# Two token tiles of a projection side by side in one PSUM bank

## The chip, the cores and the metric

The kernel runs on one core of one Trainium2 chip. The metric is the device time of one execution in microseconds. A profiled execution additionally leaves a trace of all engines: TensorE (PE, with its weight loads shown apart as PEld), VectorE (DVE), ScalarE (ACT), GpSimd (POOL) and SyncE (SP, which here issues DMAs).

## What is computed

Two layers of a bidirectional trunk over 512 tokens of 1024 features, in float32. The first layer mixes tokens with an SSD scan and an mLSTM scan, the second with a GLA scan; each is followed by a convolutional feed-forward network.

```
for i in range(DEPTH):                       # 2 layers
    h = _rmsnorm(x, norm_g[i, 0])
    if i % 2 == 0:
        h = _ssd_mlstm_mixer(h, ab_w_in, ...)    # z, xbc, dt, q, k, v, o, gates = split(h @ w_in)
    else:
        h = _gla_mixer(h, c_w_in, ...)           # q, k, v, r, g_lr = split(h @ w_in)
    x = x + _rmsnorm(h, norm_g[i, 1])
    f = _conv_ffn(_rmsnorm(x, norm_g[i, 2]), ...)
    x = x + _rmsnorm(f, norm_g[i, 3])
```

What matters here are the input projections `h @ w_in`. Of their column blocks, `z`, `v` and `o` of the first layer and `v` and `r` of the second are wanted with the tokens on the partitions; all others with the features on the partitions.

## The kernel before

Every projection is made in an emulated float32: activations and weights are each split into a high and a low part, and one product becomes three matmuls (`mm3`: high-high, high-low, low-high) that add into the same PSUM region.

The projections with tokens on the partitions are made by `nat_job` (line 452). One call takes 256 columns of weights and makes a tensor of 512 tokens by 256 columns, in four tiles `c` = 0 to 3 of 128 tokens. For a tile, the 128 tokens of `h` are the stationary operand and the 256 weight columns stream; over eight blocks of features that is 8 x 3 = 24 matmuls of 128x256. Then `post` reads the tile out of PSUM on ACT: `post_v` and `post_o` of `pair` (lines 979 and 984) with two activations of 128x128 each, `post_z` (line 795), `post_v` of layer two (line 1224) and `post_r` (line 1234) with one of 128x256.

There are 20 calls of `nat_job`, so 80 tiles and 40 pairs of tiles. In the order of `A_ORDER` = p0 x0 z0 p1 x1 z1 p2 p3 these are: `v` and `o` of head pair 0, two calls for `z0`, `v` and `o` of pair 1, two calls for `z1`, `v` and `o` of pairs 2 and 3; and in the second layer four calls of `v_proj` and four of `r_proj`. The texts below number the calls from 0 to 19 in this order.

PSUM has eight banks of 512 columns per partition, given out under three names: `pj` (2 banks, the projections), `ps` (3 banks) and `pm` (3 banks, the scans). Of `pj`, tile `c` of a `nat_job` takes one bank of 512 columns and fills 256 of them, so the two banks go back and forth from tile to tile. The jobs with features on the partitions (`run_full`: 128x512 matmuls) take banks of `pj` too.

Three streams are woven into one program by `weave` (line 47): `stream_a`, the projections, on TensorE; `stream_b`, the gates (`gate_rows`) and the SSD scan; `stream_c`, the mLSTM scan. The second layer weaves two head streams with its projections likewise. A scheduler then sets the final order of each engine by its own estimate of when things are ready, and each engine works through its instructions strictly in that order: an instruction that waits holds up all behind it on its engine. The scheduler also places the semaphore waits. In the profile all lines of the engines' calls are that of a helper, L105, so instructions are told apart by the names of their tiles: a matmul of `nat_job` is `pj<-hi,s` or `pj<-lo,s`, its read-out `s<-pj,scol`, `s<-pj,hcol` or `t<-pj,scol`.

Of the kernel before, what the change touches and what calls it, by code (L numbers as in the profile page):

```python
# [19 lines left out]
KD = 8  # L20
# [110 lines left out]
def kernel(ctx: ExitStack, tc: tile.TileContext, xin, wst, cst, dsk, gw2, out, life=None, plan=None):  # L131
# [25 lines left out]
    def ps(tag="ps"):  # L157
        uid[0] += 1
        return pp.tile([P, 512], F32, tag=tag, name=f"{tag}{uid[0]}", bufs=BANKS[tag])

    def pj():
        return ps("pj")
# [110 lines left out]
    def w_take(n, width=P):  # L273

        res = []
        for _ in range(n):
            c0 = wstate["unit"]
            i, o = divmod(c0, 1024)
            while len(wstate["ready"]) < i + 1 + W_AHEAD and wstate["next"] < NSLAB:
                w_prep()  # L280
            hi, lo = wstate["ready"][i]
            res.append((hi[:, o:o + width], lo[:, o:o + width]))
            wstate["unit"] += width
        return res

    def mm3(o, a, b, first, last, parts=False):

        (ah, al), (bh, bl) = a, b
        kw = {"skip_group_check": True} if parts else {}
        PE.matmul(o, ah, bh, start=first, stop=False, **kw)  # L290
        PE.matmul(o, ah, bl, start=False, stop=False, **kw)
        PE.matmul(o, al, bh, start=False, stop=last, **kw)

    def hp(on):
        return tc.high_priority() if on else nullcontext()
# [156 lines left out]
    def nat_job(h, post, hi=False):  # L452

        w = w_take(KD, 256)
        for c in range(NCH):
            o = pj()
            for k in range(KD):
                hh, hl = h[k]
                tk = slice(c * P, (c + 1) * P)
                mm3(o[:, :256], (hh[:, tk], hl[:, tk]), w[k], k == 0, k == KD - 1)  # L460
            with hp(hi):
                post(o[:, :256], c)
            yield

    def transpose(o, i, n=P):
# [163 lines left out]
    def mixer0(h, x_again, sc, chain_of):  # L629
# [164 lines left out]
        def z_proj(nb):  # L794
            def post_z(o, c):
                gg, hf = divmod(nb, 2)
                if hf == 0:
                    zt[c][gg] = st()
                zz = t256()
                S.activation(zz, o, AF.Identity, scale=sc.col[:, c:c + 1])  # L800
                th = t256()
                S.activation(th, zz, AF.Tanh, scale=0.5)
                V.scalar_tensor_tensor(zt[c][gg][:, hf * 256:(hf + 1) * 256], th, 1.0, zz, ALU.add, ALU.mult)
            yield from nat_job(h, post_z, False)
# [166 lines left out]
        def pair(i):  # L971
            yield from run_full([Job(h, post=post_cp(kT, 2 * i + e, P ** -0.5)) for e in range(2)])
            yield from run_full([Job(h, post=post_cp(qT, 2 * i + e, 1.0)) for e in range(2)])
            for e in range(2):
                vx[2 * i + e] = st(w=516).rearrange("p (c l) -> p c l", l=129)
                G.memset(vx[2 * i + e][:, :, 128:129], 1.0)
                ot[2 * i + e] = st()

            def post_v(o, c):
                for e in range(2):  # L980
                    S.activation(vx[2 * i + e][:, c, 0:P], o[:, e * P:(e + 1) * P], AF.Identity,
                                 scale=sc.col[:, c:c + 1])

            def post_o(o, c):
                for e in range(2):
                    S.activation(ot[2 * i + e][:, c * P:(c + 1) * P], o[:, e * P:(e + 1) * P], AF.Tanh,
                                 scale=hcol[:, c:c + 1])
            yield from nat_job(h, post_v, False)
            yield from nat_job(h, post_o, False)
            done.add(f"pair{i}")  # L990
# [617 lines left out]
```

## Time and profile before

| | |
|---|---|
| time, median of 3 runs (range) | 1539.5 us (1535.16 to 1539.62) |
| time of the profiled execution | 1537.51 us |
| its span, first to last instruction | 1535.8 us |
| PE busy | 1487.3 us, 97% of the span |
| PEld busy | 1305.5 us, 85% |
| DVE busy | 1157.0 us, 75% |
| ACT busy | 770.3 us, 50% |
| POOL busy | 141.1 us, 9% |
| HBM traffic | 104 GB/s over the span |
| mean granted TensorE clock | 0.989 |
| chain that ended last, by engine | PE 80%, DVE 13%, ACT 3%, issue 2%, DMA 2% |

How to read it. The chain is followed back from the last instruction, at each step to what released it or to the instruction ahead of it on its engine. The busy time of PE is modelled per matmul and matmuls overlap; a matmul's price is better read from start to start. The number in brackets behind a row of the timeline is the time for which the engine sat idle before it, and what ended that.

### The profile page before, as it was taken

Reading aid. Unit: us, or ns where it says so; the run is one execution under the profiler, and the core shown is the slowest. Engines: PE = TensorE matmul, PEld = TensorE weight load, DVE = VectorE, ACT = ScalarE, POOL = GpSimd, SP = SyncE. Lnnn points to the kernel's source line nnn. Section 1 sums busy time; section 2 is a strip of 40 time slices with the busy share of each in tenths; the row PEclk is TensorE's granted clock in tenths of the full one; section 3 lists DMA queues with packets and bytes.
Section 4 is the critical chain, followed back from the end, with each engine's and each line's share of the span. In section 5 each row is a group of like instructions: output and inputs, shape, how many; then the busy total and the mean of one; then the engine's idle time right before and its main releaser. Section 6 shows DMA issues by size and latency. Waiting matters only on the chain.

```text
span 1535.8 us, 23362 instructions
## 1 busy us (share of the span) xinstructions
PE 1487.3 (97%) x9008; PEld 1305.5 (85%) x9008; DVE 1157.0 (75%) x1975; ACT 770.3 (50%) x1420; POOL 141.1 (9%) x165
## 2 busy tenths in 40 slices
PE   7999998999999999999999999999999999999996
PEld 7889887887887988898898887899998889889876
DVE  7986889867764789868886686938537996889765
ACT  7445546653742655444444464637545554444433
POOL 4010311221110020000000020000003000000000
PEclk9999999999999999999999998999999999999998
DMA  6243334334331533143233432221233324222432
GB/s 199 88 160 91 107 97 127 106 93 132 110 120 47 173 98 122 55 138 97 69 105 121 137 116 90 82 70 56 69 120 128 110 69 132 89 86 77 141 94 72
DMA packets 76528, 160.96 MB, mean 105 GB/s; under 512 B 7280, under 2 KB 42112, under 8 KB 76416
## 3 DMA queue, kind: packets, MB, share of 16 engines
q1 hardware_dynamic: 66592, 149.97, 30.5%
q10 hardware_dynamic: 9360, 8.43, 1.8%
q8 instruction: 71, 1.16, 0.3%
q0 software_dynamic: 464, 1.06, 0.2%
q14 instruction: 41, 0.34, 0.1%
HBM read 150.62 MB, written 8.78 MB: 104 GB/s over the span
## 4 chain that ended last, share of the span: by engine, by line
PE 80%; DVE 13%; ACT 3%; issue 2%; DMA 2%; POOL 0%; DVEq 0%; SPq 0%; ACTq 0%; POOLq 0%
PE pj L105 33%; PE ps L105 24%; PE pm L105 23%; DVE s L105 9%; DVE lo L105 2%; ACT s L105 1%; DMA s<-rowd 1%; DVE t L105 1%; DVE pacc L105 1%; DMA raw<-in_w 0%; ACT hi L105 0%; POOL s L105 0%; DMA xsave<-s 0%; ACT t L105 0%; DVE sum L105 0%
## 5 line engine op out<-in xcount | busy, mean ns | idle before, releaser
L105 PE MATMUL pj<-s,hi 128*128 128x512 f32 (+1 forms) x1216 | 365.8, 382 | 3.5 <-ACT s L105 3.5
L105 DVE TENSOR_TENSOR lo<-raw,hi 128x1024 fp32r<-128x1024 f32 x202 | 250.8, 1246 | 111.1 <-ACT hi L105 110.6
L105 ACT CAST hi<-raw 128x1024 fp32r<-128x1024 f32 x202 | 210.6, 1047 | 213.4 <-PE pj L105 102.9
L105 PEld LDWEIGHTS pj<-s,hi 128*128 128x128 f32 x1216 | 221.6, 190 | 49.1 <-issue 5.1
L105 PE MATMUL pm<-s,hi 128*128 128x512 f32 (+1 forms) x928 | 251.6, 355 | 9.0 <-ACT s L105 7.8
L105 PE MATMUL pj<-hi,s 128*128 128x256 f32 x1280 | 243.3, 288 | 6.7 <-DVE s L105 3.7
L105 PE MATMUL ps<-s,hi 128*128 128x512 f32 (+1 forms) x928 | 245.7, 350 | 0.2 <-DVE t L105 0.2
L105 PE MATMUL pj<-s,lo 128*128 128x512 f32 (+1 forms) x608 | 230.6, 379 | 0.0
L105 PEld LDWEIGHTS pj<-hi,s 128*128 128x128 f32 x1280 | 201.6, 191 | 9.3 <-DVE s L105 4.1
L105 PEld LDWEIGHTS pm<-s,hi 128*128 128x128 f32 x928 | 164.8, 190 | 36.0 <-ACT s L105 8.7
L105 PEld LDWEIGHTS ps<-s,hi 128*128 128x128 f32 x928 | 161.7, 188 | 24.9 <-issue 0.3
L105 PE MATMUL pj<-lo,s 128*128 128x256 f32 x640 | 181.6, 284 | 0.0
L105 DVE TENSOR_TENSOR s<-s,s 128x512 f32<-128x512 f32 (+3 forms) x262 | 159.9, 630 | 18.9 <-ACT s L105 15.5
L105 DVE SCALAR_TENSOR_TENSOR s<-s,cc,s 128x511 f32<-128x511 f32 (+1 forms) x240 | 166.9, 712 | 5.3 <-ACT s L105 3.5
L105 PE MATMUL ps<-s,lo 128*128 128x512 f32 (+1 forms) x464 | 162.9, 351 | 1.2 <-DVE lo L105 1.2
L105 PE MATMUL pm<-s,lo 128*128 128x512 f32 (+1 forms) x464 | 163.4, 352 | 0.0
L105 ACT ACTIVATE s<-s 128x512 f32<-128x512 f32 (+2 forms) x153 | 91.3, 606 | 116.9 <-DVE s L105 105.2
L105 ACT ACTIVATE s<-s,cc 128x512 f32<-128x512 f32 (+2 forms) x188 | 120.7, 662 | 41.1 <-DVE s L105 39.9
L105 PEld LDWEIGHTS pj<-s,lo 128*128 128x128 f32 x608 | 115.7, 190 | 22.7 <-issue 1.3
L105 PEld LDWEIGHTS pj<-lo,s 128*128 128x128 f32 x640 | 122.5, 191 | 1.4 <-issue 1.0
L105 POOL TENSOR_TENSOR s<-s,s 128x512 f32<-128x512 f32 (+1 forms) x56 | 70.5, 1264 | 404.1 <-DVE s L105 235.6
L105 PEld LDWEIGHTS ps<-s,lo 128*128 128x128 f32 x464 | 87.3, 188 | 14.1 <-DVE lo L105 1.6
(659 smaller groups left out, 2102.0 us busy)
## 6 DMA issues: line engine op xcount, KB each, us to landing
raw<-in_w SPq DMA_DIRECT2D x234, 512.0 KB, 3.4
s<-rowd SPq DMA_DIRECT2D x64, 256.0 KB, 3.8
xmid<-s SPq DMA_DIRECT2D x32, 128.0 KB, 1.8
s<-xmid ACTq DMA_DIRECT2D x32, 128.0 KB, 2.7
s<-in_x SPq DMA_DIRECT2D x8, 256.0 KB, 5.8
s<-in_x ACTq DMA_DIRECT2D x16, 128.0 KB, 2.7
xsave<-s SPq DMA_DIRECT2D x16, 128.0 KB, 1.8
s<-xsave ACTq DMA_DIRECT2D x16, 128.0 KB, 2.6
```

The source lines that it names most:

```text
L105: return f(*a, **k)
```

## The change

`nat_job` asks for a bank only at every second tile. The even tile fills columns 0 to 255 of it, the odd tile columns 256 to 511. The number of matmuls, their shapes, the read-outs and their sizes stay as they are, and so do the numbers of banks given to each name; a call now takes two banks of `pj`, where it took four in turn.

```diff
         w = w_take(KD, 256)
         for c in range(NCH):
-            o = pj()
+            if c % 2 == 0:
+                bank = pj()
+            o = bank[:, c % 2 * 256:c % 2 * 256 + 256]
             for k in range(KD):
                 hh, hl = h[k]
                 tk = slice(c * P, (c + 1) * P)
-                mm3(o[:, :256], (hh[:, tk], hl[:, tk]), w[k], k == 0, k == KD - 1)
+                mm3(o, (hh[:, tk], hl[:, tk]), w[k], k == 0, k == KD - 1)
             with hp(hi):
-                post(o[:, :256], c)
+                post(o, c)
             yield
```

The scheduler makes another order of it. Three places show what moves.

On PE, in call 0 (`v` of pair 0), before: the second tile (`pj75`) ends, and the third (`pj76`) begins with a wait for the first tile's bank.

```order
L105 MATMUL pj75_695<-lo9_554,s24_156 128x256
L105 MATMUL pj75_695<-hi9_553,s25_157 128x256
L105 MATMUL pj76_722<-hi8_520,s10_128 128x256 [waits PE_49,Activation_49]
L105 MATMUL pj76_722<-lo8_521,s10_128 128x256
L105 MATMUL pj76_722<-hi8_520,s11_129 128x256
L105 MATMUL pj76_722<-hi8_520,s12_132 128x256
```

The same call after the change, where the first tile of bank `pj74` ends and the second tile of the same bank begins:

```order
L105 MATMUL pj74_668<-hi9_553,s25_157 128x256
L105 MATMUL pj75_721<-hi8_520,s10_128 128x256 [waits DVE_49]
L105 MATMUL pj75_721<-lo8_521,s10_128 128x256
L105 MATMUL pj75_721<-hi8_520,s11_129 128x256
L105 MATMUL pj75_721<-hi8_520,s12_132 128x256
L105 MATMUL pj75_721<-lo8_521,s12_132 128x256
L105 MATMUL pj75_721<-hi8_520,s13_133 128x256
L105 MATMUL pj74_668<-hi8_520,s10_128 128x256 [waits Activation_49]
L105 MATMUL pj74_668<-lo8_521,s10_128 128x256
```

What moved: the odd tile's first matmul now waits for ACT, whose last word on that bank is the read of the even tile that has just ended; six matmuls of the third tile (bank `pj75`) have been put between. Before, a whole tile of 24 matmuls lay between the end of a tile and the next use of its bank.

On ACT, in call 1 (`o` of pair 0), before: the reads of the first two tiles stand ahead of `dec`, a small activation of the gate rows that waits for DVE, and the third behind it.

```order
L105 ACTIVATE s71_652<-pj78_788,hcol61_516 128x128 [waits PE_49]
L105 ACTIVATE s73_655<-pj78_788,hcol61_516 128x128
L105 ACTIVATE s128_1253<-s128_1253 64x512 [waits DVE_49]
L105 ACTIVATE s71_652<-pj79_815,hcol61_516 128x128 [waits PE_49]
L105 ACTIVATE s73_655<-pj79_815,hcol61_516 128x128
L105 ACTIVATE dec129_1257<-ce127_1245 64x4
L105 ACTIVATE dec129_1257<-sC148_1394 64x4 [waits DVE_49]
L105 ACTIVATE s71_652<-pj80_842,hcol61_516 128x128 [waits PE_49]
L105 ACTIVATE s73_655<-pj80_842,hcol61_516 128x128
```

The same rows after the change:

```order
L105 ACTIVATE s71_652<-pj76_786,hcol61_516 128x128 [waits PE_49]
L105 ACTIVATE s73_655<-pj76_786,hcol61_516 128x128
L105 ACTIVATE s122_1247<-s122_1247 64x512 [waits DVE_49]
L105 ACTIVATE dec123_1251<-ce121_1239 64x4
L105 ACTIVATE dec123_1251<-sC140_1386 64x4 [waits DVE_49]
L105 ACTIVATE s71_652<-pj76_786,hcol61_516 128x128 [waits PE_49]
L105 ACTIVATE s73_655<-pj76_786,hcol61_516 128x128
L105 ACTIVATE s71_652<-pj77_839,hcol61_516 128x128 [waits PE_49]
L105 ACTIVATE s73_655<-pj77_839,hcol61_516 128x128
```

What moved: the second read of the call now stands behind `dec` too.

On PE, at the end of call 1, before: the fourth tile (`pj81`) ends, and the next job with features on the partitions (`pj95`, 128x512) waits for its bank, the one of the third tile.

```order
L105 MATMUL pj81_869<-lo11_620,s24_156 128x256
L105 MATMUL pj81_869<-hi11_619,s25_157 128x256
L105 MATMUL pj95_944<-s10_128,hi12_658 128x512 [waits PE_49,Activation_49]
L105 MATMUL pj95_944<-s11_129,hi12_658 128x512
L105 MATMUL pj95_944<-s10_128,lo12_659 128x512 [waits DVE_49]
```

After the change, from the end of the call's second tile (`pj76`) to the begin of its fourth:

```order
L105 MATMUL pj76_786<-hi11_619,s25_157 128x256
L105 MATMUL pj77_839<-lo11_620,s24_156 128x256
L105 MATMUL pj77_839<-hi11_619,s25_157 128x256
L105 MATMUL ps144_1406<-ident_74,s81_915 128x128 [waits DVE_49]
L105 MATMUL ps144_1406<-ident_74,s81_915 128x128 x3
L105 MATMUL ps145_1412<-ident_74,s82_916 128x128 [waits DVE_49]
L105 MATMUL pj91_940<-s10_128,hi12_658 128x512 [waits PE_49,Activation_49]
L105 MATMUL pj91_940<-s11_129,hi12_658 128x512
L105 MATMUL pj77_839<-hi10_586,s10_128 128x256 [waits Activation_49]
L105 MATMUL pj77_839<-lo10_587,s10_128 128x256
```

What moved: the call's fourth tile (the lower `pj77` rows) stands behind two matmuls of the next job, whose bank waits for the read of the second tile, and five transposes of the gate rows stand ahead of that wait.

## Rows read from the trace of the kernel before

**Rows 1.** The page: busy time by engine, and the chain by engine.

```profile
PE 1487.3 (97%) x9008; PEld 1305.5 (85%) x9008; DVE 1157.0 (75%) x1975; ACT 770.3 (50%) x1420; POOL 141.1 (9%) x165
...
PE 80%; DVE 13%; ACT 3%; issue 2%; DMA 2%; POOL 0%; DVEq 0%; SPq 0%; ACTq 0%; POOLq 0%
```

**Rows 2.** Waits of PE: us in total, times, longest us.

```profile
PE pj L105 <- ACT s L105: 5.3, 4, 3.5
PE pj L105 <- DVE s L105: 3.7, 2, 2.1
```

**Rows 3.** The chain in order of time (start, us): two tiles of `nat_job` back to back.

```profile
192.80 5.75 PE pj L105 x48
```

**Rows 4.** Timeline (start us, us): ends of tiles in calls 0 and 3.

```profile
63.49 0.40 PE L105 MATMUL pj<-hi,s 128*128 128x256 f32 x2
...
63.81 0.63 ACT L105 ACTIVATE s<-pj,scol 128x128 f32<-128x128 f32 x2 [2.02 <-PE pj L105]
...
119.67 0.40 PE L105 MATMUL pj<-hi,s 128*128 128x256 f32 x2
...
119.98 0.47 ACT L105 ACTIVATE t<-pj,scol 128x256 f32<-128x256 f32 x1 [1.11 <-PE pj L105]
```

**Rows 5.** Timeline: the end of call 1.

```profile
86.35 0.20 ACT L105 ACTIVATE dec<-sC 64x4 f32<-64x4 f32 x1 [7.56 <-DVE sC L105]
86.57 0.63 ACT L105 ACTIVATE s<-pj,hcol 128x128 f32<-128x128 f32 x2
...
87.25 0.73 PE L105 MATMUL pj<-s,hi 128*128 128x512 f32 x2 [3.51 <-ACT s L105]
```

**Rows 6.** Timeline: call 4, end of its third tile.

```profile
179.28 0.28 PE L105 MATMUL pj<-hi,s 128*128 128x256 f32 x1
179.40 1.88 PE L105 MATMUL ps<-s,s 128*128 128x512 f32 x4
...
182.08 0.61 ACT L105 ACTIVATE s<-pj,scol 128x128 f32<-128x128 f32 x2
```

**Rows 7.** Timeline: call 6, end of its third tile, and the begin of call 7.

```profile
259.05 0.40 PE L105 MATMUL pj<-hi,s 128*128 128x256 f32 x2
...
263.00 0.46 ACT L105 ACTIVATE t<-pj,scol 128x256 f32<-128x256 f32 x1
...
263.50 0.38 PE L105 MATMUL pj<-hi,s 128*128 128x256 f32 x1 [1.32 <-ACT t L105]
```

**Rows 8.** Timeline: ends of the third tiles of calls 8 and 9.

```profile
328.29 0.28 PE L105 MATMUL pj<-hi,s 128*128 128x256 f32 x1
...
330.31 0.60 ACT L105 ACTIVATE s<-pj,scol 128x128 f32<-128x128 f32 x2
...
342.69 0.28 PE L105 MATMUL pj<-hi,s 128*128 128x256 f32 x1
...
344.85 0.61 ACT L105 ACTIVATE s<-pj,hcol 128x128 f32<-128x128 f32 x2
```

**Rows 9.** Timeline: call 10, end of its first tile.

```profile
386.85 0.28 PE L105 MATMUL pj<-hi,s 128*128 128x256 f32 x1
...
389.25 0.58 PE L105 MATMUL pj<-hi,s 128*128 128x256 f32 x1 [2.12 <-DVE s L105]
...
392.23 0.40 ACT L105 ACTIVATE s<-s,s 128x128 f32<-128x128 f32 x1 [1.92 <-DMA s<-rowd]
392.53 0.61 ACT L105 ACTIVATE s<-pj,scol 128x128 f32<-128x128 f32 x2
```

**Rows 10.** Timeline: call 12, end of its third tile, and the begin of call 13.

```profile
978.22 0.40 PE L105 MATMUL pj<-hi,s 128*128 128x256 f32 x2
...
981.74 0.46 ACT L105 ACTIVATE s<-pj,scol 128x256 f32<-128x256 f32 x1
...
982.25 0.39 PE L105 MATMUL pj<-hi,s 128*128 128x256 f32 x1 [0.90 <-ACT s L105]
```

**Rows 11.** Windows: stretch, length, busy us (x) of PE, PEld, DVE, ACT, POOL, PEclk, DMA.

```profile
389.04:392.44 3.40, 3.19 (x15) 3.19 (x16) 3.19 (x8) 1.48 (x6) 0.00 (x0) 0.50 0.58 150
```

## The prediction

> **What bounds the kernel now.** I read the page first. PE is busy for 97% of the span and makes 80% of the chain that ended last [rows 1], so a microsecond in which PE stands still is a microsecond of the time, except in the fifth of the chain that runs over DVE, ACT and DMAs. Next the waits of PE: those before matmuls into `pj` are short and few, 5.3 us for ACT and 3.7 us for DVE [rows 2]. Then the chain in order of time, for the price of the work that the change touches: 48 matmuls of 256 columns, two tiles, take 5.75 us [rows 3], so 0.12 us a matmul and 2.87 us a tile. Last the timeline at the ends of tiles [rows 4 to 10], where the reader is to see how long after a tile's last matmul ACT has finished reading it. In a row with x2 the first of the two is the tile's last matmul, and the other already belongs to the next tile.
>
> **What the change removes and adds.** The matmuls and the reads are the same, so there is no work to price. Only waits move. Before, a bank came back after a whole tile on the other bank, 2.87 us; that sufficed nearly everywhere. Now the odd tile goes into the bank that ACT is just reading, and by the new order its first matmul waits for that read. What PE does meanwhile is what the scheduler has put between: the rows of the order count as cover, at 0.12 us each for matmuls of 256 columns. So for each of the 40 odd tiles the price is (end of ACT's read of the even tile, plus 0.05 us until PE starts, as from 87.20 to 87.25 [rows 5]) less (start of the even tile's last matmul, plus 0.12 us, plus the cover). That the wait guards the whole bank and not the columns is what the order shows; in the trace of before no matmul writes a bank that is being read. The Trainium skill says the same of the chip, in "PSUM — Partial Sum Buffer", section "PSUM bank collisions raise a hardware error": TensorE and a reader must be kept apart by bank and quadrant of partitions, not by address. By that rule the odd tile must wait, and the sum is the one below; by a rule on columns it would not wait at all and the sum would be zero.
>
> **Odd tiles where ACT is idle.** A read of two activations ends 0.95 us after the tile's last matmul begins (63.49 to 64.44), one of a single activation 0.78 us (119.67 to 120.45) [rows 4]; PE could go on after 1.00 and 0.83 us. The order gives call 0 six matmuls of cover, so 7 x 0.12 = 0.84 us, a wait of 0.16 us; nine further tiles, in calls 2, 3 and 12 to 16, have five, 0.72 us, a wait of 0.11 us. Together 2 x 0.16 + 9 x 0.11 = 1.3 us. This is the floor, and it has one answer.
>
> **Call 1.** Before, PE had all four tiles done and idled for 3.51 us until ACT, held by `dec` waiting for DVE, had read the third tile at 87.20 [rows 5]. In the new order the second read stands behind `dec` as well, and the fourth tile behind a wait for it. The gate rows on DVE do not hang on these tiles, so `dec` comes when it came; then at 87.25 PE has a whole tile left, 2.87 us, and meets a further wait of some 0.2 us, as two activations of together 0.63 us read the third tile while two matmuls run. The five transposes that now fall into the idle time give back some 0.6 us. Net 2.5 us.
>
> **Tiles where ACT is late.** Here the read of an even tile was late and nobody cared.
> - Call 4, third tile: last matmul at 179.28, read done at 182.69 [rows 6]. The cover is two float32 matmuls of 512 columns, four records of together 1.88 us, which end at 181.28, and one short matmul. Wait 182.74 - 181.3 = 1.4 us.
> - Call 6, third tile: last matmul at 259.05, read done at 263.46 [rows 7]. Cover seven matmuls: until 260.0. Wait 3.5 us, of which PE already spent 1.32 us before call 7. Net 2.2 us.
> - Calls 8 and 9, third tiles: 328.29 to 330.91, and 342.69 to 345.46 [rows 8]. For the first the cover is eight short matmuls, at least 9 x 0.12 = 1.1 us, so at most 1.6 us are left; I take 1.3. For the second it is the same pair as in call 4, 2.0 us from the last matmul on, so 0.8 us; I take 1.0, as the pair's records overlap.
> - Call 10, first tile: ACT waits for the landing of a row of `rowd` until 392.23 and reads the tile until 393.14 [rows 9]. Before, PE went on at 389.25 with the second tile; now it cannot before 393.19. What it did in that time at half clock (PEclk 0.50 in [rows 11]) was all but two matmuls of a tile, 22 x 0.12 = 2.6 us at full clock. Net 2.6 us, as long as the DMA lands when it landed.
> - Call 12, third tile: 978.22 to 982.20 [rows 10]. Cover seven matmuls, until 979.2. Wait 3.1 us, of which 0.90 us was there before. Net 2.2 us.
>
> The remaining 22 odd tiles have a longer cover or an even tile that was read early. Some reads of calls 5, 11 and 13 were late too, but by an ACT that in the new order has caught up while PE waited a tile earlier; I take zero, and up to 6 us for the upper end (that each costs again what calls 4, 10 and 12 cost: 1.4 + 2.6 + 2.2).
>
> **The clock.** In the 3.40 us from 389.04, behind PE's idle 2.12 us, the granted clock is 0.50, the lower of its two levels, 1.2 instead of 2.4 GHz [rows 9, 11]; such a stretch costs half of itself, 1.7 us. The new waits of calls 1, 6, 10 and 12 are longer than 2.12 us; calls 1 and 10 had the idle time and call 6 the smaller part of it. I count one stretch more than before, +1.7 us, with none to six for the range.
>
> **The sum.** 1.3 + 2.5 + 1.4 + 2.2 + 1.3 + 1.0 + 2.6 + 2.2 = 14.5 us, with the clock 16.2 us. From this I take 1 us, as a PE that comes later finds DVE and ACT further on, and a few of its other waits (each 0.4 to 2 us) shrink. Against the profiled execution, 1537.5 us, that gives 1552.7; the median of the runs, 1539.5, lies 2.0 above it, so the forecast for the median is 1539.5 + 15.2, some **1555 us**.
>
> **Rivals.**
> - *All waits in full.* ACT does not catch up (+6.2), the idle time already there in calls 6 and 12 is not credited (+2.2), and six waits of over 1 us drop the clock instead of one (+8.5): 15.2 + 16.9 = 32, so 1572 us. For it: the waits come in clusters within one mixer. Against: ACT is busy half of the time only [rows 1]. The Trainium skill, "TensorE: Matmul & The Clock Gate", section "A second HAM failure mode: psum-queue depth-cycling", tells of a kernel whose short idle times between PSUM banks kept bringing the clock down and up; that is this rival's mechanism, and 389 us is the place of before that agrees.
> - *The delays are absorbed.* The waits fall where the chain runs over DVE and ACT, and only the floor and call 1's remainder stay: 1.3 to 4 us, 1541 to 1543 us. For it: a fifth of the chain is not PE's, and the lateness in calls 8 to 10 comes from DMAs and DVE that PE may find further on. Against: PE has 97% and hardly any waits to give back.
> - *Faster: the bank comes back two tiles later.* When PE changes the bank, the other bank's last read now lies a tile and a half back, so the waits of PE before `pj` go, 5.3 + 3.7 us [rows 2], and two half-clock stretches behind them, 3.4 us: less 12.4, plus the floor 1.3, gives 1539.5 - 11 = 1528 us. It decides at ACT's lateness: it holds if ACT reads an even tile within the cover of 0.7 to 0.8 us. Rows 6 to 10 speak against it, and so does the order in call 1, where the 3.51 us wait stays.
> - That the odd tile does not wait after all is excluded by the order: it names ACT in 39 of 40 cases.
>
> **How the numbers follow.** A measurement of this kernel can tell some 0.3% from no change, 4.6 us. The forecast, +5 to +25 us, gets 0.65; all waits in full, above that, 0.17; absorbed, 0.13; faster, 0.05. So faster 0.05, same 0.13, slower 0.82. For 8 in 10 the range takes in the forecast's own, half of the absorbed case and most of the case in full: 1541 to 1574 us.
>
> **What would show it.** Right: the timeline of the changed kernel has PE idle at the seams inside a bank, released by ACT's read of `pj`, with PE's waits for `s` and `t` of ACT before `pj` summing to some 20 to 25 us instead of 5.3 [rows 2]; seams of calls 14 to 16 show 0.1 us; call 1's fourth tile stands behind 87 us. PE's busy time grows only by half-clock stretches. Wrong: such waits stay below 8 us in total (ACT had caught up everywhere), or PE's other waits shrink by as much as these grow.

## The result, and the profile after

The changed kernel takes 1554.26 us (median of 4 runs, 1548.81 to 1554.61), the kernel before beside it 1537.33 us (4 runs, 1533.68 to 1539.62). The ratio is 1.0106, with a 95% interval of 1.0087 to 1.0126: slower by 13 to 19 us. The forecast was 1555 us, slower, in a range of 1541 to 1574.

The profiled execution took 1554.04 us, with a span of 1552.3; before it was 1537.51 and 1535.8. From the page of after: busy time by engine; the chain by engine; and the costliest group on PE (busy us, mean ns of one | idle us just before it, and what ended most of that).

```profile
PE 1493.4 (96%) x9008; PEld 1307.5 (84%) x9008; DVE 1158.8 (75%) x1975; ACT 770.9 (50%) x1420; POOL 140.8 (9%) x165
...
PE 77%; DVE 13%; ACT 4%; DMA 3%; issue 2%; POOL 1%; SPq 0%; DVEq 0%; ACTq 0%; POOLq 0%
...
L105 PE MATMUL pj<-hi,s 128*128 128x256 f32 x1280 | 248.4, 290 | 17.2 <-ACT s L105 11.5
```

The work is the same to the instruction [rows 1], yet PE is busy for 6.1 us more and stands still for some 10 us more (a sum over all its gaps of 49.5 us instead of 39.8). The 1280 matmuls of this group now have 17.2 us of idle time in front of them. The waits of PE before `pj` name the cause (us in total, times, longest us); they answer to [rows 2]:

```profile
PE pj L105 <- ACT s L105: 15.6, 9, 4.5
PE pj L105 <- ACT t L105: 3.4, 3, 2.8
...
PE pj L105 <- DVE s L105: 2.3, 2, 1.6
```

`s` and `t` of ACT are the read-outs of `nat_job`. Waits for them sum to 19.0 us; before, those for `s` were 5.3 and those for `t` 1.3.

**Where in the program.** The clearest way to read such a change is to take one instruction that both traces have and compare its start. The first matmul that needs `pacc` closes a mixer. After (start us, us, [idle before <- releaser]):

```profile
552.60 0.38 PE L105 MATMUL ps<-ones,pacc 128*128 128x1 f32 x2 [1.19 <-DVE pacc L105]
...
1178.85 0.49 PE L105 MATMUL ps<-ones,pacc 128*128 128x1 f32 x3 [1.82 <-DVE pacc L105]
```

Before:

```profile
540.78 0.38 PE L105 MATMUL ps<-ones,pacc 128*128 128x1 f32 x2 [1.18 <-DVE pacc L105]
...
1163.85 0.49 PE L105 MATMUL ps<-ones,pacc 128*128 128x1 f32 x3 [1.83 <-DVE pacc L105]
```

PE is 11.8 us late at the end of layer 1's mixer, which has calls 0 to 11 of `nat_job`, and 15.0 us late at the end of layer 2's, which has calls 12 to 19. The end of PE's work is 15.85 us later. So three quarters of the loss is made in the first 550 us, and between the mixers nothing is given back.

**A seam where ACT is idle.** A seam is the change from the even to the odd tile inside a bank. Here it is the end of an even tile in call 3 of after (timeline; start us, us), the kind of place that [rows 4] show of before. The even tile's last matmul began at 124.19, and five matmuls of another bank are cover:

```profile
124.51 0.47 ACT L105 ACTIVATE t<-pj,scol 128x256 f32<-128x256 f32 x1 [0.52 <-PE pj L105]
...
124.77 0.28 PE L105 MATMUL pj<-lo,s 128*128 128x256 f32 x1
125.03 0.39 PE L105 MATMUL pj<-hi,s 128*128 128x256 f32 x1
125.26 0.28 PE L105 MATMUL pj<-lo,s 128*128 128x256 f32 x1
```

The read ends at 124.98, the odd tile starts at 125.03. Without the wait it would have started 0.12 us after 124.77, so 0.14 us are lost. But the next matmul follows only 0.23 us later, where 0.12 is the pace. The weight loads of the same kind of seam in call 0 show why:

```profile
64.33 0.19 PEld L105 LDWEIGHTS pj<-hi,s 128*128 128x128 f32 x1 [0.20 <-ACT s L105]
64.44 0.19 PEld L105 LDWEIGHTS pj<-lo,s 128*128 128x128 f32 x1
```

The odd tile's first matmul starts at 64.33, and the load of its own weights, held by the same wait, only then too; elsewhere a load starts 0.12 us ahead of its matmul (63.81 and 63.93, for one). So the load for the second matmul starts 0.11 us behind, and that matmul another 0.11 us later, at 64.55. A wait drains the overlap between loads and matmuls, and filling it again costs 0.11 us on top. A seam costs 0.25 us.

**Call 1** in the timeline of after, to be read beside [rows 5]:

```profile
86.17 0.20 ACT L105 ACTIVATE dec<-sC 64x4 f32<-64x4 f32 x1 [8.01 <-DVE sC L105]
86.40 1.14 ACT L105 ACTIVATE s<-pj,hcol 128x128 f32<-128x128 f32 x4
...
87.08 1.22 PE L105 MATMUL pj<-s,hi 128*128 128x512 f32 x2 [4.01 <-ACT s L105]
...
88.10 0.41 PE L105 MATMUL pj<-hi,s 128*128 128x256 f32 x1
```

ACT has stood behind `dec` for 8.01 us, `dec` comes when it came before (86.35 then), and the second and third tile are read behind it. PE idles 4.01 us instead of 3.51, and the whole fourth tile still has to be done. In the windows of after (stretch, length, busy us (x) of PE, PEld, DVE, ACT, POOL, PEclk, DMA share, GB/s), half-clock time covers the idle time:

```profile
83.90:87.08 3.18, 0.00 (x0) 0.00 (x0) 2.66 (x8) 0.88 (x4) 0.97 (x2) 0.50 0.18 39
87.08:90.73 3.65, 3.65 (x15) 3.46 (x16) 1.38 (x2) 2.10 (x5) 1.28 (x3) 0.50 0.37 96
```

PE had no matmul in the first 3.18 us of them; the 3.65 on work stand beside 3.41 before, so the clock costs about the same in both. The first matmul of call 2 comes 2.72 us later than before. After:

```profile
108.31 0.28 PE L105 MATMUL pj<-hi,s 128*128 128x256 f32 x1
```

Before:

```profile
105.59 0.28 PE L105 MATMUL pj<-hi,s 128*128 128x256 f32 x1
```

By then five transposes are done that before came later, so the loss of calls 0 and 1 is some 2.3 us. The 0.3 us that call 0 loses at its seams adds nothing to it, as PE waits for `dec` anyway.

**The late reads.** PE in the timeline of after, in call 2 (the first two rows), at the end of an even tile of call 4 and the begin of the odd tile behind it, and in call 6 ([rows 6, 7] are such places of before):

```profile
111.99 0.39 PE L105 MATMUL pj<-hi,s 128*128 128x256 f32 x1 [0.67 <-DVE s L105]
...
113.19 0.39 PE L105 MATMUL pj<-hi,s 128*128 128x256 f32 x1 [0.34 <-ACT t L105]
...
183.62 0.28 PE L105 MATMUL pj<-hi,s 128*128 128x256 f32 x1
...
187.36 0.39 PE L105 MATMUL pj<-hi,s 128*128 128x256 f32 x1 [1.62 <-ACT s L105]
...
270.06 0.39 PE L105 MATMUL pj<-hi,s 128*128 128x256 f32 x1 [2.82 <-ACT t L105]
```

At 183.62 the last matmul of an even tile begins, as at 179.28 in [rows 6], and the odd tile follows at 187.36: the cover ends with a wait of 1.62 us for ACT. In call 6 the wait is 2.82 us.

Call 10 in the timeline of after, beside [rows 9]:

```profile
395.51 1.05 PE L105 MATMUL pm<-s,s 128*128 128x128 f32 x8
...
400.13 0.40 ACT L105 ACTIVATE s<-s,s 128x128 f32<-128x128 f32 x1 [1.74 <-DMA s<-rowd]
400.44 0.61 ACT L105 ACTIVATE s<-pj,scol 128x128 f32<-128x128 f32 x2
...
401.10 0.40 PE L105 MATMUL pj<-hi,s 128*128 128x256 f32 x1 [4.54 <-ACT s L105]
```

The first tile is done at 395.51, but ACT, in its fixed order, first waits for the DMA of a row of `rowd` until 400.13, then reads until 401.05. PE has nothing but eight short matmuls and stands for 4.54 us. Before, it did the second tile in that time.

### The profile page after: what moved, and what is told of

It reads as the page before. It is cut to its first block, busy times and chain, and to the rows that moved or that the text cites. A ratio compares the mean times of both kernels' runs of the same rounds, so it can differ in the third digit from the quotient of the medians.

```text
span 1552.3 us, 23339 instructions
## 1 busy us (share of the span) xinstructions
PE 1493.4 (96%) x9008; PEld 1307.5 (84%) x9008; DVE 1158.8 (75%) x1975; ACT 770.9 (50%) x1420; POOL 140.8 (9%) x165
## 4 chain that ended last, share of the span: by engine, by line
PE 77%; DVE 13%; ACT 4%; DMA 3%; issue 2%; POOL 1%; SPq 0%; DVEq 0%; ACTq 0%; POOLq 0%
PE pj L105 30%; PE ps L105 23%; PE pm L105 23%; DVE s L105 9%; DMA s<-rowd 3%; ACT s L105 2%; DVE lo L105 2%; DVE t L105 1%; ACT hi L105 1%; POOL s L105 1%; DVE pacc L105 0%; DMA raw<-in_w 0%; ACT L105 0%; ACT t L105 0%; DVE rd L105 0%
## 5 line engine op out<-in xcount | busy, mean ns | idle before, releaser
L105 PE MATMUL pj<-hi,s 128*128 128x256 f32 x1280 | 248.4, 290 | 17.2 <-ACT s L105 11.5
```

What stands on the lines that cost most here:

```text
L105: return f(*a, **k)
```

## The experiments

The theory to be tested has three parts: the loss comes from the odd tile following the even one into a bank that is still to be read, and not from packing as such; it is made mostly at the places where ACT reads late; and the floor at the other seams is small. The rivals: packing itself costs (fewer banks in flight, another order of everything), or the floor is the main thing. The kernels stand against the kernel before of the same chip by their ratios; the two groups of experiments ran on two chips (before: 1535.5 and 1536.73 us).

**Same packing, tiles in another order.** The two banks take turns again, with tiles 0, 2, 1, 3.

```
-        for c in range(NCH):
-            if c % 2 == 0:
-                bank = pj()
-            o = bank[:, c % 2 * 256:c % 2 * 256 + 256]
+        banks = [pj(), pj()]
+        for c in (0, 2, 1, 3):
+            o = banks[c // 2][:, c % 2 * 256:c % 2 * 256 + 256]
```

> Two tiles to a bank as in the changed kernel, but made in the order 0, 2, 1, 3, the two banks in turn, so that a whole tile on the other bank (24 matmuls) lies between a tile and the next one in its bank. Theory A (PE waits for ACT's read inside the bank, because a tile's 0.8 to 1.0 us of reading, or ACT's lateness, has only 0.7 to 0.8 us of cover): the time is that of the kernel before within 0.3%, 1533 to 1542 us, and PE's waits for ACT before pj sum to 5 to 8 us as before. Rival B (that a call holds two banks instead of four, or that an odd tile lies in the upper half of a bank, costs the time): 1549 to 1555 us. Rival C (the scheduler's new order as such, not the wait, costs it): neither, a time between.

Measured: 1532.12 us (11 runs, 1529.45 to 1536.47), ratio 0.9975 (0.9961 to 0.9988): the loss is gone, as the theory of the bank order expects, down to 1 us below its range. Its waits of PE:

```profile
PE pj L105 <- ACT s L105: 6.0, 4, 3.5
...
PE pj L105 <- DVE s L105: 3.4, 3, 1.6
...
PE pj L105 <- ACT t L105: 1.3, 1, 1.3
```

These are [rows 2] again, the 3.5 us at call 1 among them. Two tiles in one bank cost nothing; the whole loss, 1.3% against this kernel, lies in the order in which the banks are reused. Set against the trace of before by equal work (each matmul weighed by its spacing at full clock, 0.118 us for 256 columns and 0.232 for 512; then the times are compared at which both have done the same sum), it is 0.1 us late at the end of layer 1's mixer and 0.5 early at 900 us, then 5.0 early from 950 us to the end: the 4.5 us between are a stretch at half clock that the trace of before has and this one has not, and which is told of at the end. The other runs say the same: an estimate of a run's time at full clock is its span times its mean granted clock (good to some 1 us, as the clock is on record to 0.001), and the median of this is 1520.1 us here (11 runs) and 1520.2 before (23 runs). So its 0.25% need no gain of the packing; they are a higher granted clock (median 0.993 instead of 0.991), and why it is higher is open. The Trainium skill, "Perfetto Trace Analysis", section "Matmuls", asks to rotate independent groups of matmuls through different PSUM banks so that the read-out of one lies beside the matmuls of the next; this pair of runs agrees, and puts 1.3% on it.

**Same order as in the change, reads behind the odd tile.** Nobody reads a bank before both tiles are in it.

```
-            with hp(hi):
-                post(o, c)
+            if c % 2 == 1:
+                with hp(hi):
+                    post(bank[:, :256], c - 1)
+                    post(bank[:, 256:], c)
```

> Two tiles to a bank in the order 0, 1, 2, 3 as in the changed kernel, but the two reads are issued together after the odd tile, so no matmul waits for a read inside a bank, and a bank comes back after two tiles, 5.7 us, instead of one. Theory A: no waits inside a bank; the waits that the kernel before had at the change of banks (3.5 us after call 1, 1.3 us before call 7, 0.9 us before call 13) shrink too, so 1529 to 1537 us, 0 to 8 us under the kernel before. Rival B (two banks a call, or upper halves, cost the time): 1549 to 1555 us. Rival D (later reads hold up those who use v, o, z and r): 1540 to 1550 us, with longer waits of PE before ps and pm.

Measured: 1524.27 us (6 runs, 1522.89 to 1530.47), ratio 0.9934 (0.9916 to 0.9952): faster than before by 7 to 13 us, and 5 us below the range expected. This is the prediction's rival "the bank comes back two tiles later", which needs this edit to come true. Its waits of PE:

```profile
PE ps L105 <- DVE s L105: 6.3, 3, 3.6
...
PE pj L105 <- ACT s L105: 1.3, 1, 1.3
```

And its timeline, in call 1 and at the end of call 6:

```profile
83.52 0.63 PE L105 MATMUL pj<-s,hi 128*128 128x512 f32 x2
...
90.58 0.73 PE L105 MATMUL pj<-s,hi 128*128 128x512 f32 x2 [1.32 <-ACT s L105]
...
265.10 0.69 PE L105 MATMUL ps<-s,s 128*128 128x64 f32 x2 [3.59 <-DVE s L105]
```

PE leaves call 1 at 83.52 without a wait, where before it went on at 87.25 [rows 5]: the bank that the next job takes has been read by then. Of the 10.7 us of waits before `pj` in the kernel with swapped tiles, 1.5 us are left. A part comes back elsewhere: waits before `ps` for DVE, 2.5 us there, are 6.3 here, the longest at 265.10, as PE now reaches the recurrence before DVE. By equal work against the trace of before, PE is 3.8 us early behind call 1, 5.0 at the end of layer 1's mixer, 4.5 more behind the half-clock stretch of before that is no doing of this edit, another 2.9 behind call 12, where the wait of 0.90 us [rows 10] is gone too, and 13.0 at the end. Without the stretch that is some 8.5 us. The medians say 10, and 8.0 by span times granted clock (1512.2 instead of 1520.2).

**The change in one layer only.** `nat_job` gets an argument that says whether two tiles share a bank; the first kernel packs in layer 1, the second in layer 2.

```
-            if c % 2 == 0:
+            if c % 2 == 0 or not pack:
                 bank = pj()
-            o = bank[:, c % 2 * 256:c % 2 * 256 + 256]
+            o = bank[:, c % 2 * 256:c % 2 * 256 + 256] if pack else bank[:, :256]
```

> Two tiles to a bank in the first layer alone (calls 0 to 11); the second layer as before. In the trace of the changed kernel PE runs 11.8 us behind the kernel before when layer 1 is done. Theory A (a sum of local waits): 10 to 14 us over the kernel before. Rival C (the order of the whole program decides): no such split.

> Two tiles to a bank in the second layer alone (calls 12 to 19). Theory A: 2.0 us at call 12 and 13 and some 0.25 us at each of the seams with an idle ACT, 3 to 5 us over the kernel before, and together with the first layer alone the 16.9 us of the whole change. Rival C: no such split.

Measured: layer 1 alone 1549.61 us (4 runs, 1548.31 to 1553.69), ratio 1.0098 (1.008 to 1.0115), so +15.0 us; layer 2 alone 1540.67 us (10 runs, 1536.87 to 1542.76), ratio 1.0032 (1.0021 to 1.0043), so +4.9 us. The sum, 19.9 us with about 3.2 to either side, and the whole, 16.3 with 3 to either side, overlap. Part of it is the clock: by span times granted clock layer 1 alone is 8.4 us over the kernel before and layer 2 alone 3.3. Layer 1 cost 1 us more than expected and has the waits:

```profile
PE pj L105 <- ACT s L105: 14.5, 9, 4.4
...
PE pj L105 <- ACT t L105: 3.6, 3, 2.3
```

With the change in layer 2 only:

```profile
PE pj L105 <- ACT s L105: 7.2, 4, 3.5
```

Of the 7.2 us, call 1's 3.5 were there before. Layer 2 has the regular `v` and `r` projections, and adds a quarter of the whole.

**The floor alone.** The change's order stands only in six calls where ACT reads soon (calls 2, 3 and 13 to 16), the swapped order everywhere else; the diff is against the kernel with swapped tiles. `near` says whether the call's number is in `NEAR`; left out of the cut are the counter of calls and that a bank is asked for at its first tile, not both at the begin of the call.

```
+NEAR = (2, 3, 13, 14, 15, 16)
-        for c in (0, 2, 1, 3):
+        for c in (0, 1, 2, 3) if near else (0, 2, 1, 3):
```

> The kernel with the tile order 0, 2, 1, 3, but calls 2, 3 and 13 to 16 in the order 0, 1, 2, 3 of the changed kernel: the calls in which ACT is idle when an even tile ends, 12 seams inside a bank. To be read against the order 0, 2, 1, 3 everywhere, 1532.1 us. Theory A with the price of the trace of the changed kernel (0.13 us of wait that the cover leaves, and 0.11 us more before the second matmul, as the next weights were not loaded ahead): 12 x 0.25 = 3.0 us, and some 1 us in call 2, whose cover waits for DVE: 1535 to 1537 us. The prediction's price (0.11 us a seam, nothing behind it): 1.3 us, 1533.5 us.

Measured: 1538.27 us (12 runs, 1534.29 to 1542.79), ratio 1.0013 (0.9997 to 1.0029). Against the swapped order's 0.9975 that is +0.38%, 5.8 us with about 3.2 to either side, for twelve seams; the range expected reached to 1537 us. By the prediction's 0.11 us a seam it would be at most 1.3 us, below that interval. But not all of the 5.8 us is seams. By span times granted clock it is 2.7 us (1523.1, where before is 1520.5; the swapped order lies 0.1 below its own); the other 3 us go with the granted clock, whose median is 0.991 here and 0.993 with swapped tiles. And one of the twelve seams was not of the kind meant: in call 13 ACT was late after all. Its timeline:

```profile
983.10 0.46 ACT L105 ACTIVATE s<-pj,scol 128x256 f32<-128x256 f32 x1
...
983.61 0.39 PE L105 MATMUL pj<-hi,s 128*128 128x256 f32 x1 [1.45 <-ACT s L105]
```

The even tile's last matmul began at 981.21. Nine of the other eleven show in the timeline, eight with 0.23 to 0.25 us (start to start, against the pace) and one with 0.39, so the 0.25 us of the changed kernel holds here too. With call 13 that makes 4.1 us; a part comes back, as the wait of 0.60 us for DVE that the swapped tiles have in call 2 is not here.

**The late calls alone.** The same with `NEAR = (0, 1, 4, 5, 6, 7, 8, 9, 10, 11, 12)`.

> The counterpart: calls 0, 1 and 4 to 12 in the order 0, 1, 2, 3, in which ACT is late or held, and 0, 2, 1, 3 in all others. Theory A (most of the cost is ACT's lateness at a few places): 12 to 16 us over the order 0, 2, 1, 3 everywhere, 1544 to 1548 us, and with e5_idle the whole of the change, 22 us over 1532.1. Rival E (the cost is spread evenly over the 40 seams): 22 of them, so 12 of 22 us, with waits of equal length.

Measured: 1550.94 us (6 runs, 1549.29 to 1552.5), ratio 1.0095 (1.0078 to 1.0113): +1.2% over the swapped order, 18.4 us with about 3.3 to either side, where 12 to 16 were expected. Waits of PE:

```profile
PE pj L105 <- ACT s L105: 15.7, 11, 4.5
...
PE pj L105 <- ACT t L105: 3.1, 1, 3.1
```

That is the waits of the whole change. The two experiments together (calls 17 to 19 are in neither), 24.2 us with about 5.5 to either side, stand beside 20.1 for the whole change over the swapped order (1.0106 less 0.9975, with 3.6 to either side): the parts add up as far as the runs can tell, and three quarters of the sum are the calls of this experiment. With the clock taken out as above they are 2.7 and 10.4 us, four fifths in the late calls. So somewhat more than half of what was measured here is lost at full clock, and the rest goes with a lower granted clock; how much of that the waits bring about is not shown. Rival E, an even spread, would put 22 of the 34 seams' cost here, 65%; the times alone hardly tell that from three quarters, the lengths of the waits do: up to 4.5 us here, and 0.25 at most seams of the experiment before.

**One late call alone.** `NEAR = (10,)`: call 10, where a DMA holds ACT.

> The order 0, 1, 2, 3 in call 10 alone, 0, 2, 1, 3 in all others. The prediction's term for this place: PE waits some 5 us for ACT, which is held by the landing of a row of rowd, and loses 2.6 us against the kernel before. Theory A: one wait of 4 to 5 us in the trace and 2 to 4 us over the 1532.1 us of the order 0, 2, 1, 3. Rival F (such a wait is given back by the other streams): a wait of 4 to 5 us, and less than 1 us.

Measured: 1535.96 us (12 runs, 1534.21 to 1539.06), ratio 0.9996 (0.9983 to 1.0009): +0.21%, 3.2 us with about 2.8 to either side; the prediction's price is 2.6. The interval does not exclude rival F, less than 1 us. Its timeline at call 10:

```profile
390.33 0.40 ACT L105 ACTIVATE s<-s,s 128x128 f32<-128x128 f32 x1 [1.64 <-DMA s<-rowd]
...
391.30 0.39 PE L105 MATMUL pj<-hi,s 128*128 128x256 f32 x1 [4.36 <-ACT s L105]
```

The wait of 4.54 us of the changed kernel stands there by itself, at 4.36, with the same releaser and the same DMA ahead of it, though nothing else in the kernel waits in the new way. It does not need the delays of the calls before. Against rival F stands the trace: by equal work against the swapped tiles, PE loses 4.4 us between 380 and 430 us, of which 1.7 belong to a stretch at half clock behind the wait that the swapped tiles do not have there, and up to 930 us nothing of it comes back.

## Why the prediction was right, and which of its steps were not

The forecast's time and sign held, and so did the mechanism: with the banks in turns the loss is gone, and the calls with late reads carry most of it. To compare the terms, the delay of PE by equal work is read from the two traces behind each group of calls: 0.3 us (call 0), 2.3 (call 1), 4.3 (call 3), 6.8 (call 5), 6.0 (at 300 us, behind call 7), 8.9 (call 9), 8.5 (before call 10), 11.1 (call 10), 11.8 (call 11), 13.9 (call 12), 15.0 (call 19), 15.9 (end). By groups, in us:

| calls | predicted | measured |
|---|---|---|
| 0 and 1 | 2.8 (0.3 of it floor) | 2.3 |
| 2 and 3 | 0.4 (floor) | 2.0 |
| 4 and 5 | 1.4 | 2.5 |
| 6 and 7 | 2.2 | -0.8 |
| 8 and 9 | 2.3 | 2.9 |
| up to call 10 | | -0.4 |
| 10 | 2.6 | 2.6 |
| 11 | 0 | 0.7 |
| 12 | 2.2 | 2.1 |
| 13 to 19 | 0.6 (floor) | 1.1 |
| behind them | | 0.9 |
| clock, in no one place | 1.7 | about 1.8, contained in the rows above |
| given back, in no one place | -1.0 | contained in the rows above |
| all | 15.2 | 15.9 on PE, 16.5 in the span |

- **Call 1: right.** Place, releaser and time (88.10, "behind 87 us") came as said, and 2.3 us for calls 0 and 1 stand beside 2.8; the floor of call 0 vanishes in the wait.
- **Late reads: right in three places.** Calls 8, 10 and 12 lie within 0.3 us of their price. The way to it was the same each time: end of ACT's read, less the end of the cover that the order shows, less what PE had idled there before. It held also where the cause sat two steps away, as with the DMA in call 10. In call 12 it can be read from the timeline of after: the wait of 0.90 us before call 13 [rows 10] is still there, and one of 1.81 is new ahead of it. The prediction had one wait of 3.1 us less those 0.90, so its net of 2.2 is right and its split is not:

```profile
992.14 0.38 PE L105 MATMUL pj<-hi,s 128*128 128x256 f32 x1 [1.81 <-ACT s L105]
...
994.09 0.39 PE L105 MATMUL pj<-hi,s 128*128 128x256 f32 x1 [0.87 <-ACT s L105]
```

- **Call 9: wrong, and hidden in the row.** Of the 2.9 us for calls 8 and 9, 1.6 come at call 8's third tile (wait of 1.35 us at 338.35, predicted 1.3). The wait of 1.0 us at call 9's third tile did not come: ACT, which before began to read 2.16 us after the tile's last matmul had begun (342.69 to 344.85 [rows 8]), does so after 0.54 us here (351.59 to 352.13), and the odd tile starts 1.32 us behind the begin of its cover (351.70), as the fourth tile did before (342.80 to 344.12):

```profile
352.13 0.61 ACT L105 ACTIVATE s<-pj,hcol 128x128 f32<-128x128 f32 x2
...
353.02 0.68 PE L105 MATMUL pj<-hi,s 128*128 128x256 f32 x1
```

  The other 1.2 us are lost in small pieces ahead of call 8's wait, which no term had. That the row comes near its price is luck.
- **Call 6, and what is given back: mis-sized.** The wait came, 2.82 us where 3.5 was said. But the term credited one wait of before, the 1.32 us ahead of call 7 [rows 7], and a second one stood behind it, in the timeline of before:

```profile
267.70 1.10 PE L105 MATMUL ps<-s,s 128*128 128x64 f32 x8 [1.81 <-DVE s L105]
```

  A PE that comes later finds DVE done, and this one is gone too: 1.32 + 1.81 is more than 2.82. "A few of its other waits shrink" named it, at 1 us for the whole kernel; in calls 6 and 7 alone the term is 3.0 us less than predicted. Here the rival "absorbed" holds.
- **The floor: mis-sized.** The wait of 0.11 to 0.16 us was right, 0.14 in the trace. The step that failed is to take the wait for the loss: each also costs the 0.11 us of refilling weight loads. "PE's busy time grows only by half-clock stretches" failed with it. It grew by 6.1 us; some 1.8 of it is the clock. The rest fits the waits: at full clock 24 matmuls of `nat_job` show the refill behind a wait in the trace of after, 4 in that of before, and at each the profile shows some 0.26 us of lost time as busy, together some 5 us. These are 0.11 us of refill (the matmul at 125.03 is shown with 0.39 us, a lone one with 0.28) and 0.16 us ahead of the wait, as the last matmul before it is shown with 0.28 us where the next would have started after 0.12.
- **Calls 2 and 3: mis-sized**, as the prediction took the cover's matmuls as free to run. Beside four seams at 0.25 us, in call 2 the cover itself waits 0.67 us for DVE, still busy with the job before (111.99 above), and the odd tile another 0.34 behind it.
- **Calls 4, 5 and 11: too low.** The third tile of call 4 waits 1.62 us instead of 1.4, plus its seams; calls 5 and 11 were put at zero, "up to 6 us for the upper end", and cost 0.5 and 0.7.
- **The clock: right in sum.** Stretches at half clock last 23.9 us in the trace of before and 30.7 in that of after, 3.2 of these on an idle PE; half of the 3.6 more on work is 1.8 us, where 1.7 was said. The place is luck: the rival's six further stretches did not come, and the one that is new is not behind a wait for `pj`, but behind the 1.82 us wait for `pacc` at the end of layer 2's mixer, where the trace of before has a wait of 1.83 us and no such stretch; in the windows of after:

```profile
1179.60:1182.90 3.30, 3.30 (x18) 3.30 (x17) 1.58 (x6) 0.45 (x2) 0.00 (x0) 0.50 0.00 0
```

- **Sum of the waits:** "some 20 to 25 us" for `s` and `t` of ACT was 19.0, just under; below 8 would have been wrong.

So the total is nearer than its parts deserve: the floor, call 2's cover and calls 4, 5 and 11 came out some 4 us above their price, and calls 6 and 7 three below theirs, while call 9's missing wait was made up by losses that nobody had priced.

## What to carry to other kernels

Before two tiles share a PSUM bank, ask when its reader runs, not how many banks are saved: if tiles are taken in bank order, PE waits for every late read of the even tile, and a read is late wherever its engine's queue stands behind a gate row or a DMA. The same packing with the banks in turns lost nothing, and with both reads behind the second tile it gave 0.7%, as a bank is then asked for again only two tiles later and the waits for it nearly vanish (1.5 us of 10.7). When pricing a short wait of PE, add the refill of the weight loads behind it, and see whether the work that should cover it can itself run.

## What the runs showed of the hardware

**A wait of PE costs 0.11 us more than it lasts**: 0.23 us from the first matmul to the second instead of 0.12, with the second weight load issued only behind the first (64.33 and 64.44 above). The idle time in the brackets of the timeline leaves out another 0.16 us, as it counts from the shown end of the matmul ahead, 0.28 us behind its start.

**A stretch of 10.2 us at half clock while PE is never idle, in some traces only.** Windows (stretch, length, busy us (x) of PE, PEld, DVE, ACT, POOL, PEclk, DMA share, GB/s) of the same piece of work, before:

```profile
930.00:938.60 8.60, 8.60 (x38) 5.53 (x36) 7.06 (x12) 4.75 (x6) 0.00 (x0) 1.00 0.48 172
938.60:948.80 10.20, 10.20 (x23) 6.61 (x22) 4.41 (x7) 1.39 (x3) 0.00 (x0) 0.50 0.14 51
```

The trace of after has it too, from 950.90 to 961.10 with 23 matmuls. With swapped tiles:

```profile
938.60:948.80 10.20, 10.20 (x41) 6.50 (x39) 8.54 (x13) 3.30 (x6) 0.00 (x0) 1.00 0.27 86
```

23 matmuls instead of 41 in the same time; by equal work between before and the swapped order, 4.5 us lost. It is absent from the traces of the first four experiments. Those with the floor alone and with call 10 alone have a shorter one of 6.8 us at the same piece of work; the first of them:

```profile
937.80:944.60 6.80, 6.80 (x16) 4.49 (x15) 2.83 (x5) 0.63 (x1) 0.00 (x0) 0.50 0.22 77
```

PE is shown as busy throughout, in the 8.60 us ahead of the long one and the 7.80 us ahead of this one too, so no idle time right ahead of it brings it; what does is open. There is one trace of each kernel, so that it differs between executions of one kernel is not shown by traces, but it fits the spread of single runs (five of the six with deferred reads took 1522.9 to 1524.8 us at a granted clock of 0.993 or 0.994, one 1530.5 us at 0.989). It is the reason why the experiments are compared by medians and ratios, and traces only piece by piece.
